# A fourth seven-product pair in seven feed-forward units, three low halves added by DMA, later transposes and a longer load ring

## The chip, the cores and the metric

One core of a Trainium2 chip runs the whole program. The metric is the device time of one execution in microseconds (us); the median of the runs of the kernel before is 1593.85 us (three runs, 1590.32 to 1594.32). The engines are called as in the profile: PE (matrix products, with PEld for its weight loads), DVE (vector), ACT (scalar functions), POOL (GpSimd) and SP, which here only issues DMAs. Each of them runs its instructions in the order in which the program puts them, and waits at an instruction until what it needs is there.

## The reference

A transformer layer over 256 rows of width 2048, in 32-bit floats: a normalisation with shift, scale and gate from a conditioning vector `c`, three token mixers over one projection, an output projection, and a gated feed-forward part of width 5632.

```python
mod = silu(c) @ w_ada + b_ada
shift1, scale1, gate1, shift2, scale2, gate2 = split(mod, 6)
h = rms_norm(x, norm1_gain) * (1 + scale1) + shift1
x = x + gate1 * mixing_sublayer(h, ...)     # stick-breaking, dilated, gated linear attention
h = rms_norm(x, norm2_gain) * (1 + scale2) + shift2
gate, up = split(h @ w_ffn_in, 2)
x = x + gate2 * ((silu(gate) * up) @ w_ffn_out)
```

## The kernel before

**Products.** Every 32-bit operand is split into a high part of reduced precision and the remainder, its low half. A product is three matmuls (`mm3`, lines 162 to 166): high by high, high by low (line 165, which reads the low half of the weights), low by high. A matmul has 128 rows of depth, 128 rows of the activation and 512 columns of weights.

**Weights.** A tile of weights is 256 rows by 512 columns, 512 KB. SP loads it into a raw room (four of them, tag `raw`). ACT casts it to the high part (line 158 in `load_weights`, 1305 in `split` of `load_pair`), and DVE subtracts the high part from the raw tile to give the low half (lines 159 and 1306). These results go to four rooms `whi`/`wlo`; in units 1 to 7 of the feed-forward part two more pairs of rooms (`more_rooms`, the tags A2/A3 and A4/A8, shown as A) join them, in a fixed rotation of six. A room is free again when PE has read it, a raw room when ACT and DVE have.

**The feed-forward part.** It runs in 11 units of 512 gate columns and the 512 up columns that belong to them; the depth of 2048 is taken as 8 pairs of 128-row chunks. Units 0 and 8 to 10 take the gate columns first and then the up columns, by `block`. Units 1 to 7 (`FAST`) take both at once in `fast_products`, pair by pair in the order of `PAIRS`. A plain pair p (flag 0) has a tile of gate and a tile of up columns (here "first tile" and "second tile"), and 8 products: 24 matmuls, in the order of the columns. A pair with flag 1, called fast here, treats the 2x2 blocks of activations (two row tiles by two chunks) and weights (two chunks by two column halves) by a scheme of seven products in place of eight, 21 matmuls. For it DVE makes four differences of weights in two further rooms, tags OD and KD (line 1309), and three and a half tiles are cast and split. The activations' differences that a fast pair needs are made once, in unit 0 (`sums_of_h2`). Four of the seven products go to shared PSUM banks over all fast pairs of a unit. After the last fast pair ACT and DVE combine them (lines 1380 to 1384) and DVE adds the combinations to the four outputs (`merge`, line 1340). Plain pairs behind the last fast pair add to the same outputs.

Behind a unit, ACT takes the sigmoid of the gate half (line 1419), DVE multiplies (lines 1420 and 1429), and in the next unit, between its first and its second pair, PE transposes the result with eight small matmuls (`turn`, line 1119), ACT and DVE splitting it for the last stage. The unit's two groups of PSUM banks, acc and misc, change places from unit to unit.

Below, P0 to P4 are plain pairs, and F5 to F7 fast ones. Before: P0, P1, F5, P2, F6, F7, P3, P4.

**Mixers.** `qk_norm` scales the heads of queries and keys on DVE (line 646), and `qk_turn` transposes them on PE (line 658) with a copy by ACT (line 659). For the stick-breaking heads this happens in one go after block 5 of the projection, and the first scores (line 681) follow in `gla`, by `sb_step`, between the chunks of blocks 9 to 12. For the dilated heads it happens in steps of a block: `steps` names the chunk before which each step is put. `dil_scores` makes the scores (with an exp on ACT, line 891), `mixture` transposes the probabilities on PE (line 936), and a sigmoid of the gates stands in between on ACT, which loads another function table for it.

**Gate2.** From unit 8 on, the products of `c` with the columns of `w_ada` for gate2 run in the background, paced by `tick`. SP loads 512 KB at a time into a ring of rooms (`ring["tags"]`, three: AR0, AR1, KC), and DVE multiplies and adds (line 289). `mac` keeps at most as many loads open as the ring has rooms. The middle sum x2 is kept in DRAM meanwhile: POOL stores it by four DMAs of 512 KB in the stage before (`put_away`, line 1217), and SP brings it back into A2, A3, A4 and A8 (`bring_back`, line 1221) once the fast units are through. In the last stage (`w_ffn_out`) fast pairs are used too.

**Order.** A scheduler puts the instructions on their engines by a priority that follows the program; `prio()` raises it for loads, casts and the like, so that these come ahead. `tc.issue_after(x)` puts an instruction behind x on its engine.

Of the kernel before, what the change touches and what calls it, by code (L numbers as in the profile page):

```python
# [10 lines left out]
F32 = mybir.dt.float32  # L11
F32R = mybir.dt.float32r
U8 = mybir.dt.uint8
AF = mybir.ActivationFunctionType
ALU = mybir.AluOpType
AX = mybir.AxisListType

P = 128
T = 256
NT = T // P  # L20
D = 2048
KC = D // P
DFF = 5632
NB = 512
# [8 lines left out]
RATE_IN, RATE_MID, RATE_FFN = 0.8, 0.6, 0.65  # L33
RATE_OUT = 2.5
LOOK = 3
DEFER = 4
AHEAD = 4000
WARM = (22, 38, 13)
# [7 lines left out]
OUT_UNITS = (4, 5, 6)  # L46
OUT_A = tuple((p, 0) for p in range(8)) + tuple(x for i in range(6) for x in ((8 + i, 1), (14 + i, 0))) + ((20, 0), (21, 0))
OUT_B = ((0, 0), (1, 0)) + tuple(x for i in range(6) for x in ((8 + i, 1), (2 + i, 0)))
PAIRS = ((0, 0), (1, 0), (5, 1), (2, 0), (6, 1), (7, 1), (3, 0), (4, 0))
RANK = 16  # L50
ROW_N1, ROW_N2, ROW_SBQ, ROW_SBK, ROW_DILQ, ROW_DILK, ROW_GB, ROW_GG = 16, 32, 48, 49, 50, 51, 52, 56

# [23 lines left out]
def trunk(ctx: ExitStack, tc: tile.TileContext, I, out):  # L76
# [16 lines left out]
    def S(tag, shape, dtype=F32):  # L93
        return slot.tile(shape, dtype, tag=tag, name=nm(tag))
# [383 lines left out]
    def proj_block(g, b, w=None, carry=False, steps=None):  # L478
        k0, k1 = GROUPS[g]
        go_on = bool(carried)  # L480
        pss = carried.pop() if go_on else [acc_bank() for _ in range(NT)]
        seeded = g == LAST and not go_on
        if seeded:

            with prio():
                for t in range(NT):
                    nc.scalar.copy(pss[t], A[b][:, t, :])
            go_on = True
        block(pss, h_at, w_in, k0, k1, b * NB, w=w, go_on=go_on, more=carry, seeded=seeded, steps=steps)
# [160 lines left out]
    def qk_turn(parts, behind=None):  # L650

        for b, h0, h1, gain in parts:
            for h in range(h0, h1, 2):
                ps = misc_bank([P, NT, 2, P])
                for t in range(NT):
                    for i in range(2):
                        with tc.issue_after(behind) if behind is not None else nullcontext():
                            nc.tensor.transpose(ps[:, t, i, :], heads(b)[:, t, h + i, :], ident)
                nc.scalar.activation(heads(b)[:, :, h : h + 2, :], ps, AF.Copy, scale=gain(h))
# [62 lines left out]
    def gla():  # L722
# [19 lines left out]
        nc.scalar.copy(aT, ps[: 2 * RANK, :])  # L742

        for i, b in enumerate((9, 10, 11, 12)):
            proj_block(LAST, b, steps={1: lambda: sb_step(2 * i), 3: lambda: sb_step(2 * i + 1)})
        with tc.issue_after(state["mm"].ins), prio():
            sb_step(8)

# [264 lines left out]
        proj_block(LAST, b)  # L1013
    state["rate"] = RATE_IN
    proj_block(LAST, 5)
    qk_turn(sb_parts, state["mm"].ins)
    sb_hi, sb_lo, sb_step = stick_breaking()
    og = gla()
    for b in range(6, 9):
# [5 lines left out]

    dil_scores, dil_weights = dilated()
    dil_steps = {
        4: lambda: qk_turn(dil_parts[:2]),
        7: lambda: qk_turn(dil_parts[2:]),
        10: lambda: dil_scores(0, 3),  # L1030
        13: lambda: dil_scores(3, 6),
    }
    rr = []
    for j in range(2):
# [228 lines left out]
    def sums_of(sf, h, a, b):  # L1263

        (a0, b0), (a1, b1) = ((x[:, a, :], x[:, b, :]) for x in h)
        for dst, x, y, op in (
            (0, a1, b1, ALU.add), (2, a0, a1, ALU.subtract), (1, sf[:, 0], a0, ALU.subtract), (3, b0, sf[:, 1], ALU.subtract)
        ):
            nc.vector.tensor_tensor(sf[:, dst], x, y, op=op)

    def sums_of_h2():
        out = {}
        sf = S("AR1", [P, 4, P])
        sums_of(sf.rearrange("p s (n d) -> p s n d", n=1), [h2_raw[2, t] for t in range(NT)], slice(2, 3), slice(3, 4))
        hl = S("AR0", [P, 2, 4, P], F32R)
        nc.scalar.copy(hl[:, 0], sf)
        nc.vector.tensor_tensor(hl[:, 1], sf, hl[:, 0].bitcast(F32), op=ALU.subtract)
        out[5] = [(hl[:, 0, j, :], hl[:, 1, j, :]) for j in range(4)]
        sf = S("AR1", [P, 4, 2, P])
        sums_of(sf, [h2_raw[3, t] for t in range(NT)], slice(0, 4, 2), slice(1, 4, 2))  # L1280
        hi, lo = S("OS1", [P, 4, 2, P], F32R), S("OS2", [P, 4, 2, P], F32R)
        nc.scalar.copy(hi, sf)
        nc.vector.tensor_tensor(lo, sf, hi.bitcast(F32), op=ALU.subtract)
        for n in range(2):
            out[6 + n] = [(hi[:, j, n, :], lo[:, j, n, :]) for j in range(4)]
        return out

    def load_pair(src, p, c0, c1, fast, tags):


        def raw_at(c):
            raw = wp.tile([P, 2, NB], F32, tag="raw", name=nm("raw"))
            nc.sync.dma_start(raw, src[2 * p * P : (2 * p + 2) * P, c : c + NB].rearrange("(k p) c -> p k c", p=P))
            return raw

        def split(src):
            n = src.shape[1]
            more_rooms = state.get("more_rooms", ())
            i = state["tiles"] = (state.get("tiles", -1) + 1) % (4 + len(more_rooms))
            if i < len(more_rooms):  # L1300
                hi, lo = (S(tag, [P, 2, NB], F32R) for tag in more_rooms[i])
            else:
                hi = wp.tile([P, 2, NB], F32R, tag="whi", name=nm("whi"), bufs=4)
                lo = wp.tile([P, 2, NB], F32R, tag="wlo", name=nm("wlo"), bufs=4)
            nc.scalar.copy(hi[:, :n, :], src)  # L1305
            state["split"] = nc.vector.tensor_tensor(lo[:, :n, :], src, hi[:, :n, :].bitcast(F32), op=ALU.subtract)  # L1306
            return [(hi[:, i, :], lo[:, i, :]) for i in range(n)]

        sub = lambda dst, x, y: nc.vector.tensor_tensor(dst, x, y, op=ALU.subtract)
        with prio():  # L1310
            if not fast:
                return [split(raw_at(c0)), split(raw_at(c1))]
            r0, r1 = raw_at(c0), raw_at(c1)
            b11, b21 = split(r0)
            ta, tb = (S(tag, [P, 2, NB]) for tag in tags)
            sub(ta[:, 0], r1[:, 0], r0[:, 0])
            sub(ta[:, 1], r1[:, 1], r1[:, 0])
            (b22,) = split(r1[:, 1:2])
            sub(tb[:, 0], r1[:, 1], ta[:, 0])
            sub(tb[:, 1], r0[:, 1], tb[:, 0])  # L1320
            t1, t3 = split(ta)
            t2, t4 = split(tb)
            return b11, b21, b22, t1, t3, t2, t4
# [68 lines left out]
        return fast_products(w_ff, i * NB, DFF + i * NB, PAIRS, h2_at, h2s, own, other, ("OD", "KD"))  # L1392

    state["rate"] = RATE_FFN
    state["more_rooms"] = tuple(zip(X2_TAGS[0::2], X2_TAGS[1::2]))
    ring["tags"] = ("AR0", "AR1", "KC")
    act = []
    for i in range(NFF):
        if i in FAST:
            pg, pu = fast_unit(i)  # L1400
        else:
            pg = [acc_bank() for _ in range(NT)]
        if i == FAST[-1] + 1:
            bg.append(gate2_bg())
        if i in FAST:
            pass
        elif i == 0:
            w = load_weights(w_ff, 0, KC, 0, spare=("A12", "KD", "A9", "A10", "A0", "A1", "T1", "T2"))
            for t in range(NT):
                block(pg, h2_at, None, 0, KC, 0, w=w, tiles=(t,), steps=None if t else {N2_AT[1]: lambda: norm2_turn(1, xs)})  # L1410
        else:
            block(pg, h2_at, w_ff, 0, KC, i * NB)
        if i == 0:
            h2s = sums_of_h2()
        sgs = []
        with prio():
            for t in range(NT):
                sg = scr([P, NB])
                nc.scalar.activation(sg, pg[t], AF.Sigmoid)
                nc.vector.tensor_mul(sg, sg, pg[t])  # L1420
                sgs.append(sg)
        if i not in FAST:
            pu = [acc_bank() for _ in range(NT)]
            block(pu, h2_at, w_ff, 0, KC, DFF + i * NB)
        hi = S(ftags[2 * i], [P, 4, T], F32R)
        lo = S(ftags[2 * i + 1], [P, 4, T], F32R)
        with prio():
            for t in range(NT):
                nc.vector.tensor_mul(sgs[t], sgs[t], pu[t])  # L1429

        def turn(sgs=sgs, hi=hi, lo=lo, bank=acc_bank if i + 1 in FAST and i % 2 == 0 else misc_bank):
            for t in range(NT):
                transpose_split(sgs[t], hi, lo, t, bank)

        later.append(turn)
        act.append((hi, lo))
# [33 lines left out]


    state["rate"] = RATE_OUT
    state["more_rooms"] = ()
    hooks = {at: (lambda n=n: sums_of_unit(n)) for n, at in enumerate((2, 4, 6))}
    hooks[7] = flush

# [84 lines left out]
```

## Time and profile before

| | us |
|---|---|
| median of the runs (1590.32 to 1594.32) | 1593.85 |
| the profiled execution | 1593.15 |
| its span, first to last instruction | 1591.4 |
| PE busy | 1576.3 |
| DVE busy | 1299.3 |
| ACT busy | 850.2 |
| POOL busy | 11.2 |

The times of the page are those of the profiled execution; 1.75 us of its time lie outside the span. The granted clock of PE is at or above nine tenths in every slice of it. A PE matmul is shown with its whole duration of 0.39 us, though the next one starts 0.23 us after it; its pace is read from the starts. A row of groups gives the line, the engine, what is written and read, the shape, the count, the busy time and the mean in ns, and then the engine's idle time ahead of such instructions and what ended it.

### The profile page before, as it was taken

The page shows a single profiled execution, that of the slowest core. Times are in us where ns is not written, and L with a number is a line of the kernel's source. Part 1 is how long each engine was busy: PE and PEld are TensorE (multiplying, and loading weights), DVE is VectorE, ACT ScalarE, POOL GpSimd, SP SyncE. Part 2 cuts the span into 40 slices and gives each one's busy share as a digit, 9 for nine tenths or more (in the row PEclk, how much of TensorE's full clock was granted, in tenths as well). Part 3 has the DMA queues.
Part 4 walks back from the last instruction along what each step waited for, and adds up shares of the span by engine and source line. Part 5 has one row for each costly group of instructions (what it writes and reads, how often), then busy time and mean ns, then how long its engine had stood idle before and what let it go on. Part 6 is the DMA issues. An engine that isn't in the chain of part 4 may idle for free.

```text
span 1591.4 us, 20176 instructions
## 1 busy us (share of the span) xinstructions
PE 1576.3 (99%) x7243; PEld 1304.6 (82%) x7243; DVE 1299.3 (82%) x1556; ACT 850.2 (53%) x1193; POOL 11.2 (1%) x22
## 2 busy tenths in 40 slices
PE   8999999999999999999999999999999999999998
PEld 7878888888788888888887888888888888888887
DVE  6889996888888686877756689999997777989884
ACT  5654448775755444444445755555554444455552
POOL 1000000000000000000000000000000000000000
PEclk9999999999999999999999999999999999999999
DMA  9999997667788899988767556666668889756664
GB/s 330 357 331 322 332 305 235 220 193 248 233 273 271 297 306 316 317 283 293 230 210 240 179 185 196 194 202 196 211 189 276 283 294 313 244 185 218 205 206 139
DMA packets 195740, 400.16 MB, mean 251 GB/s; under 512 B 13038, under 2 KB 28052, under 8 KB 195640
## 3 DMA queue, kind: packets, MB, share of 16 engines
q1 hardware_dynamic: 194664, 396.70, 75.6%
q0 software_dynamic: 800, 2.11, 0.3%
q8 instruction: 57, 0.93, 0.3%
q14 instruction: 43, 0.35, 0.1%
q10 hardware_dynamic: 176, 0.07, 0.0%
HBM read 394.63 MB, written 4.19 MB: 251 GB/s over the span
## 4 chain that ended last, share of the span: by engine, by line
PE 86%; DMA 5%; DVE 5%; ACT 3%; issue 1%; SPq 0%; ACTq 0%; DVEq 0%
PE acc L166 21%; PE acc L165 21%; PE acc L164 21%; PE misc L165 6%; PE misc L166 6%; PE misc L164 6%; DMA raw<-w_ffn_out 1%; DMA AR<-w_ada 1%; DVE ada L289 1%; ACT whi L158 1%; DVE wlo L159 1%; PE misc L809 1%; DMA A<-w_ada 1%; DMA OS<-w_ada 1%; DVE wlo L1306 1%
## 5 line engine op out<-in xcount | busy, mean ns | idle before, releaser
L158 ACT CAST whi<-raw 128x1024 fp32r<-128x1024 f32 x362 | 368.6, 1022 | 411.0 <-PE acc L166 257.2
L159 DVE TENSOR_TENSOR wlo<-raw,whi 128x1024 fp32r<-128x1024 f32 x362 | 426.2, 1184 | 181.3 <-ACT whi L158 179.0
L164 PE MATMUL acc<-whi,H 128*128 128x512 f32 x1245 | 487.3, 392 | 1.4 <-ACT H L455 0.8
L165 PE MATMUL acc<-wlo,H 128*128 128x512 f32 x1245 | 486.5, 391 | 0.8 <-DVE wlo L159 0.7
L166 PE MATMUL acc<-whi,H 128*128 128x512 f32 x1245 | 485.2, 390 | 0.4 <-DVE H L462 0.4
L166 PEld LDWEIGHTS acc<-whi,H 128*128 128x128 f32 x1245 | 233.5, 188 | 50.6 <-DVE H L462 1.6
L164 PEld LDWEIGHTS acc<-whi,H 128*128 128x128 f32 x1245 | 233.7, 188 | 50.2 <-ACT H L455 1.3
L165 PEld LDWEIGHTS acc<-wlo,H 128*128 128x128 f32 x1245 | 233.8, 188 | 48.7 <-DVE wlo L159 1.7
L1305 ACT CAST whi<-raw 128x1024 fp32r<-128x1024 f32 (+1 forms) x148 | 141.9, 974 | 99.8 <-PE acc L166 40.1
L1306 DVE TENSOR_TENSOR wlo<-raw,whi 128x1024 fp32r<-128x1024 f32 (+1 forms) x148 | 162.6, 1122 | 8.1 <-ACT whi L1305 6.8
L164 PE MATMUL acc<-whi,A 128*128 128x512 f32 x222 | 87.0, 392 | 1.0 <-DVE scr L1429 1.0
L165 PE MATMUL acc<-wlo,A 128*128 128x512 f32 x222 | 86.4, 389 | 0.0
L166 PE MATMUL acc<-whi,A 128*128 128x512 f32 x216 | 84.1, 389 | 0.0
L289 DVE SCALAR_TENSOR_TENSOR ada<-AR,csil,ada 128x1024 f32<-128x1024 f32 x60 | 76.1, 1280 | 7.3 <-DMA AR<-w_ada 7.3
L165 PE MATMUL misc<-wlo,H 128*128 128x512 f32 x158 | 61.7, 390 | 0.8 <-DVE wlo L1306 0.8
L164 PE MATMUL misc<-whi,H 128*128 128x512 f32 x158 | 61.7, 391 | 0.0
L166 PE MATMUL misc<-whi,H 128*128 128x512 f32 x158 | 61.5, 389 | 0.0
L164 PEld LDWEIGHTS acc<-whi,A 128*128 128x128 f32 x222 | 41.7, 188 | 9.8 <-issue 1.4
L165 PEld LDWEIGHTS acc<-wlo,A 128*128 128x128 f32 x222 | 41.7, 188 | 8.6 <-DVE wlo L159 0.2
L1305 ACT CAST whi<-AR 128x1024 fp32r<-128x1024 f32 x24 | 25.3, 1053 | 43.6 <-PE acc L166 21.1
L1305 ACT CAST A<-raw 128x1024 fp32r<-128x1024 f32 (+1 forms) x36 | 34.9, 982 | 25.0 <-PE misc L166 8.6
L166 PEld LDWEIGHTS acc<-whi,A 128*128 128x128 f32 x216 | 40.5, 188 | 8.5
(485 smaller groups left out, 2291.0 us busy)
## 6 DMA issues: line engine op xcount, KB each, us to landing
raw<-w_in SPq DMA_DIRECT2D x205, 512.0 KB, 5.2
raw<-w_ffn_in SPq DMA_DIRECT2D x176, 512.0 KB, 4.5
raw<-w_ffn_out SPq DMA_DIRECT2D x88, 512.0 KB, 4.9
AR<-w_ada SPq DMA_DIRECT2D x79, 512.0 KB, 5.0
raw<-w_out SPq DMA_DIRECT2D x32, 512.0 KB, 4.9
KC<-w_ada SPq DMA_DIRECT2D x30, 512.0 KB, 5.2
OS<-w_ada SPq DMA_DIRECT2D x16, 512.0 KB, 6.9
KD<-w_ada SPq DMA_DIRECT2D x16, 512.0 KB, 5.5
```

Of the source, the lines that this page charges most:

```text
L158: state["cast"] = nc.scalar.copy(hi[:, :n, :], raw[:, :n, :])
L159: state["split"] = nc.vector.tensor_tensor(lo[:, :n, :], raw[:, :n, :], hi[:, :n, :].bitcast(F32), op=ALU.subtract)
L164: nc.tensor.matmul(ps, lh, rh, start=start, stop=False, skip_group_check=seeded)
L165: nc.tensor.matmul(ps, lh, rl, start=False, stop=False, skip_group_check=seeded)
L166: state["mm"] = nc.tensor.matmul(ps, ll, rh, start=False, stop=stop, skip_group_check=seeded)
L289: nc.vector.scalar_tensor_tensor(acc, raw, c, acc, op0=ALU.mult, op1=ALU.add)
L809: nc.tensor.matmul(ps[:n, t * N_GLA + h, :].rearrange("p (s l) -> p s l", l=L), at(f, h, t)[:, :n], odd(at(f, h, t)), start=True, stop=True,)
L1305: nc.scalar.copy(hi[:, :n, :], src)
L1306: state["split"] = nc.vector.tensor_tensor(lo[:, :n, :], src, hi[:, :n, :].bitcast(F32), op=ALU.subtract)
```

## The change

It has four parts.

1. Pair 4 becomes a fast pair in units 1 to 7. The order is now P0, P1, F4, P2, F5, F6, F7, P3, so three fast pairs stand in a row and one plain pair behind them. Both merges come after the last pair. `sums_of_h2` also makes the activations' differences for pair 4.
2. The second tile of P0 and both tiles of P1 in units 1 to 7 get their low halves in another way: ACT writes the negated high part into the room of the low half, and POOL issues a DMA that reads the raw weights from DRAM again and adds them there. DVE has no part in these three tiles. These are 21 DMAs of 512 KB.
3. Transposes are held: the last of three groups of stick-breaking heads (eight transposes and two copies) is moved into block 9, and the two transposing steps of the dilated heads go from chunks 4 and 7 to 7 and 10, behind the product last issued, their scores from 10 and 13 to 13 and 15.
4. The ring of gate2 loads has five rooms instead of three; A2 and A3 join it, so these two quarters of x2 come back later.

```diff
-PAIRS = ((0, 0), (1, 0), (5, 1), (2, 0), (6, 1), (7, 1), (3, 0), (4, 0))
+PAIRS = ((0, 0), (1, 0), (4, 1), (2, 0), (5, 1), (6, 1), (7, 1), (3, 0))
+ADDED = ((0, True), (1, False), (1, True))
...
         for i, b in enumerate((9, 10, 11, 12)):
-            proj_block(LAST, b, steps={1: lambda: sb_step(2 * i), 3: lambda: sb_step(2 * i + 1)})
+            steps = {1: lambda: sb_step(2 * i), 3: lambda: sb_step(2 * i + 1)}
+            if i == 0:
+                steps[2] = lambda: qk_turn(sb_parts[2:], state["mm"].ins)
+            proj_block(LAST, b, steps=steps)
...
-    qk_turn(sb_parts, state["mm"].ins)
+    qk_turn(sb_parts[:2], state["mm"].ins)
...
     dil_steps = {
-        4: lambda: qk_turn(dil_parts[:2]),
-        7: lambda: qk_turn(dil_parts[2:]),
-        10: lambda: dil_scores(0, 3),
-        13: lambda: dil_scores(3, 6),
+        7: lambda: qk_turn(dil_parts[:2], state["mm"].ins),
+        10: lambda: qk_turn(dil_parts[2:], state["mm"].ins),
+        13: lambda: dil_scores(0, 3),
+        15: lambda: dil_scores(3, 6),
     }
...
     def sums_of_h2():
         out = {}
-        sf = S("AR1", [P, 4, P])
-        sums_of(sf.rearrange("p s (n d) -> p s n d", n=1), [h2_raw[2, t] for t in range(NT)], slice(2, 3), slice(3, 4))
-        hl = S("AR0", [P, 2, 4, P], F32R)
...
+        for n in range(2):
+            sf = S("OD", [P, 4, P])
+            c = 2 * n
+            sums_of(sf.rearrange("p s (n d) -> p s n d", n=1), [h2_raw[2, t] for t in range(NT)], slice(c, c + 1), slice(c + 1, c + 2))
+            hl = S(f"AR{n}", [P, 2, 4, P], F32R)
+            nc.scalar.copy(hl[:, 0], sf)
+            nc.vector.tensor_tensor(hl[:, 1], sf, hl[:, 0].bitcast(F32), op=ALU.subtract)
+            out[4 + n] = [(hl[:, 0, j, :], hl[:, 1, j, :]) for j in range(4)]
+        sf = S("KC", [P, 4, 2, P])
...
+        def weights(c):
+            return src[2 * p * P : (2 * p + 2) * P, c : c + NB].rearrange("(k p) c -> p k c", p=P)
...
-        def split(src):
+        def split(src, again=None):
...
             nc.scalar.copy(hi[:, :n, :], src)
-            state["split"] = nc.vector.tensor_tensor(lo[:, :n, :], src, hi[:, :n, :].bitcast(F32), op=ALU.subtract)
+            if again is None:
+                state["split"] = nc.vector.tensor_tensor(lo[:, :n, :], src, hi[:, :n, :].bitcast(F32), op=ALU.subtract)
+            else:
+                nc.scalar.activation(lo, hi.bitcast(F32), AF.Copy, scale=-1.0)
+                nc.gpsimd.dma_start(lo, again, accum_op=ALU.add)
...
-                return [split(raw_at(c0)), split(raw_at(c1))]
+                return [split(raw_at(c), weights(c) if (p, c == c1) in state.get("added", ()) else None) for c in (c0, c1)]
...
     state["rate"] = RATE_FFN
+    state["added"] = ADDED
...
         if i == FAST[-1] + 1:
+            ring["tags"] = ("AR0", "AR1", "KC", "A2", "A3")
             bg.append(gate2_bg())
...
-    state["more_rooms"] = ()
+    state["more_rooms"] = state["added"] = ()
```

More of the change, by code (lines that the diff above doesn't have):

```diff
@@ L1272, in sums_of_h2 @@
         out = {}
-        sf = S("AR1", [P, 4, P])
-        sums_of(sf.rearrange("p s (n d) -> p s n d", n=1), [h2_raw[2, t] for t in range(NT)], slice(2, 3), slice(3, 4))
-        hl = S("AR0", [P, 2, 4, P], F32R)
[L1276 to L1279, printed above, removed]
+        for n in range(2):
[7 more added lines that the diff above has]
+        sf = S("KC", [P, 4, 2, P])
         sums_of(sf, [h2_raw[3, t] for t in range(NT)], slice(0, 4, 2), slice(1, 4, 2))
@@ L1288, in load_pair @@
     def load_pair(src, p, c0, c1, fast, tags):
+        def weights(c):
+            return src[2 * p * P : (2 * p + 2) * P, c : c + NB].rearrange("(k p) c -> p k c", p=P)
         def raw_at(c):
             raw = wp.tile([P, 2, NB], F32, tag="raw", name=nm("raw"))
-            nc.sync.dma_start(raw, src[2 * p * P : (2 * p + 2) * P, c : c + NB].rearrange("(k p) c -> p k c", p=P))
+            nc.sync.dma_start(raw, weights(c))
             return raw
-        def split(src):
+        def split(src, again=None):
             n = src.shape[1]
```

## The prediction

> **What bounds the kernel now.** I read the page first (busy times, chain), then PE's waits, the chain over units 1 to 7, the windows of one unit, the groups of DVE and ACT.
>
> ```profile
> span 1591.4 us, 20176 instructions
> ...
> PE 1576.3 (99%) x7243; PEld 1304.6 (82%) x7243; DVE 1299.3 (82%) x1556; ACT 850.2 (53%) x1193; POOL 11.2 (1%) x22
> ...
> PE 86%; DMA 5%; DVE 5%; ACT 3%; issue 1%; SPq 0%; ACTq 0%; DVEq 0%
> ```
>
> PE sets the end: only fewer matmuls, or shorter waits of PE, can bring time. Its waits, as total, count and longest:
>
> ```profile
> PE misc L658 <- DVE A L646: 1.8, 2, 1.1
> PE acc L164 <- DVE scr L1429: 1.0, 1, 1.0
> PE misc L658 <- ACT A L659: 0.9, 1, 0.9
> ...
> PE misc L165 <- DVE wlo L1306: 0.8, 1, 0.8
> ```
>
> None of these lies in units 1 to 7 (926.0 to 1222.7 us). There the chain is PE alone, and seven units end on the beat:
>
> ```profile
> 1010.81 0.87 PE acc L1119 x8
> ...
> 1053.18 0.87 PE misc L1119 x8
> ...
> 1222.73 0.88 PE misc L1119 x8
> ```
>
> A unit takes (1222.73 - 1010.81)/5 = 42.38 us: the turn of 0.87, and 3 fast pairs of 21 matmuls and 5 plain ones of 24, 183 in all, so 0.2268 us each. The window of one unit shows how close the others are (busy us of PE, PEld, DVE, ACT, POOL, then clock, DMA share, GB/s):
>
> ```profile
> 1010.80:1053.20 42.40, 42.40 (x194) 35.20 (x192) 39.71 (x49) 24.12 (x27) 0.00 (x0) 1.00 0.63 198
> ```
>
> DVE is busy for 39.71 us of 42.40, at a granted clock of 1.00. It is the next bound, 2.7 us away.
>
> **The change, part by part.** *Seven products for a fourth pair.* Each of seven units loses 3 matmuls: 21 x 0.2268 = **-4.76 us** if PE never waits; the unit becomes 41.70. The price is on DVE and ACT (count, busy, mean ns):
>
> ```profile
> L1306 DVE TENSOR_TENSOR wlo<-raw,whi 128x1024 fp32r<-128x1024 f32 x58 | 69.8, 1220 | 4.9 <-ACT whi L1305 4.9
> ...
> L1309 DVE TENSOR_TENSOR OD<-raw,raw 128x512 f32<-128x512 f32 x20 | 13.8, 688 | 4.7 <-DMA raw<-w_ffn_in 4.7
> ```
>
> ```profile
> L1305 ACT CAST whi<-raw 128x1024 fp32r<-128x1024 f32 x58 | 60.7, 1054 | 44.0 <-PE misc L166 15.6 <-PE acc L166 13.0 <-DMA raw<-w_ffn_in 9.1
> ```
>
> Back to back these overlap a little, so I cost DVE from start to start: 1.14 us for 1024 columns, 0.60 for 512.
>
> ```profile
> 1089.65 1.22 DVE L1306 TENSOR_TENSOR wlo<-raw,whi 128x1024 fp32r<-128x1024 f32 x1
> 1090.79 0.69 DVE L1340 TENSOR_TENSOR acc<-acc,KC 128x512 f32<-128x512 f32 x1
> 1091.39 0.68 DVE L1420 TENSOR_TENSOR scr<-scr,acc 128x512 f32<-128x512 f32 x1
> ```
>
> A fast pair needs three splits of 1024 and five operations of 512 (four differences, one split), 6.42 us; a plain one two splits, 2.28. That is +4.14 per unit. *The adding DMAs* take 3 splits (-3.42) away. DVE then has 39.71 + 0.72 = 40.43 us of work in a unit of 41.70: 1.27 us left, where it had 2.69. ACT gets one and a half casts more and three negated copies, 4.5 x 1.05 = 4.7, so 28.9 of 41.7: off the path by its sum, though each copy stands between a cast and POOL's issue.
>
> What decides is the adding DMA's time from issue to landing, L. No row shows one that adds. The nearest are POOL's four plain stores of the same 512 KB, and SP's loads of the same tiles in one unit:
>
> ```profile
> L1217 POOL DMA_DIRECT2D x<-A x4: 531/534/568, 809.6 to 876.3; - x4
> ...
> DMA to landing us min/median/max: 2.9/5.4/6.2
> ```
>
> ```profile
> L1293 SPq DMA_DIRECT2D raw<-w_ffn_in x19: 367/368/372, 1000.7 to 1046.2; - x19
> ...
> DMA to landing us min/median/max: 3.6/4.4/5.0
> ```
>
> ```profile
> q1 hardware_dynamic: 194664, 396.70, 75.6%
> ```
>
> The stores' landings follow what else is under way; their stretches (0.84 is the DMA share of the 6.2 us from 831.37, 0.61 that of the store of 2.9):
>
> ```profile
> 831.40:837.60 6.20, 6.20 (x30) 5.11 (x28) 2.94 (x3) 2.96 (x5) 0.51 (x1) 1.00 0.84 273
> ...
> 876.30:879.30 3.00, 3.00 (x15) 2.49 (x14) 1.02 (x2) 3.00 (x10) 0.53 (x1) 1.00 0.61 243
> ```
>
> A packet takes 0.756 x 16 x 1591.4 / 194664 = 0.099 us; 512 KB are 256 packets of 2 KB, 16 for each engine, 1.58 us. An add has the tile in SBUF to read as well. Bounds: 2.9 (the fastest store, the second read hidden) and 6.2 + 1.6 = 7.8 (the slowest, the second read wholly added). A unit's share grows from 0.63 to 0.63 x 19/16 = 0.75 (three tiles more than 16), between the two stores. I take 5.2: the median load of these units, 4.4, which lies between them too, and half of the second read.
>
> The budget, counted from the end of the last fast pair (F7): P3 runs to 5.45, P0 of the next unit to 10.9, the turn to 11.77, P1 to 17.2. Plain pairs take the columns in order, so the second tile's low half is read half-way: P0's at 8.4, P1's at 14.7, and P1's first at 12.0. P0's second raw tile is issued when F7's differences free its room, at -3.5, lands at about 0.8 (4.4 later), is cast by 1.85, negated by 2.95, issued at 3.05: it has 5.35 us. P1's first, issued at 5.75, has 6.2. P1's second negation stands on ACT behind both sigmoids and is issued between 9.0 and 9.9: 4.8 to 5.7. So the smallest budget is 4.8 to 5.35, and one us of L beyond it costs PE one us in each of six units (unit 1 loads these tiles while plain unit 0 runs). With L = 5.2 the stall is 0 to 0.4; I take 0.2 x 6 = **+1.2**; ends 0 and (7.8 - 5.2) x 6 = 15.6. SP's raw loads share the engines with these tiles: 198 GB/s become about 235, less than the 312 of the window from 1312 us below, where PE was still busy for 44.04 of 45.00; 0.
>
> What is queued behind: PE runs in order, so everything behind P0 or P1 slips with it. POOL has nothing else in these units. The tiles free their rooms only when PE has read them, so a stall also holds back the casts six tiles on; it doesn't add up.
>
> The Trainium skill, "DMA: Bandwidth & Descriptors", section "Anatomy of one DMA — SWDGE (gpsimd) path", fits a fixed 2.0 us plus bytes over 436 GB/s, an estimate of 3.2 us here: by it the sum has no stall. The row of 2.9 agrees, the median of 5.4 does not.
>
> *Three fast pairs in a row, one plain pair behind.* In before, DVE is ahead of PE in the last fast pair by 3.3 us: the split ends at 1074.62, and PE reads it at 1077.95.
>
> ```profile
> 1073.40 1.22 DVE L1306 TENSOR_TENSOR wlo<-KD,whi 128x1024 fp32r<-128x1024 f32 x1
> ```
>
> ```profile
> 1077.95 0.39 PE L165 MATMUL misc<-wlo,OS 128*128 128x512 f32 x1
> ```
>
> A fast pair takes PE 4.76 and DVE 6.42, so each in a row eats 1.66 of the lead: the third leaves 3.3 - 1.66 = 1.6, less what the fuller tiles hold back; following the six rooms step by step I get 0.7. Positive, so 0; the bound is in the rivals. The last product (L1429) ends 2.1 us before the turn needs it; by the same steps, 0.7; also 0.
>
> ```profile
> 1092.58 0.68 DVE L1429 TENSOR_TENSOR scr<-scr,acc 128x512 f32<-128x512 f32 x1
> ```
>
> ```profile
> 1095.41 1.04 PE L1119 MATMUL acc<-ident,scr 128*128 128x128 f32 x8
> ```
>
> *Held transposes.* For the stick-breaking heads:
>
> ```profile
> 277.32 1.84 ACT L659 ACTIVATE A<-misc,qgains 128x512 f32<-128x512 f32 x3
> ...
> 279.04 1.85 ACT L659 ACTIVATE A<-misc,vec 128x512 f32<-128x512 f32 x3
> ```
>
> ```profile
> 278.06 1.24 PE L658 MATMUL misc<-ident,A 128*128 128x128 f32 x8 [0.94 <-ACT A L659]
> ...
> 279.83 0.66 PE L681 MATMUL misc<-A,A 128*128 128x256 f32 x2
> ```
>
> The last eight transposes go behind the first two chunks of block 9, but the first scores (L681, at 279.83) need the fourth copy, which is among the first four that stay and ends at 279.04 + 1.85/3 = 279.7 either way. PE comes there sooner and waits there: the wait moves. 0, within 0.9 either way. For the dilated heads both transposes go 3 steps later, and L646's results (ready 1.1 us late at worst) are there:
>
> ```profile
> 413.62 0.39 PE L166 MATMUL acc<-whi,H 128*128 128x512 f32 x1
> 415.10 0.44 PE L658 MATMUL misc<-ident,A 128*128 128x128 f32 x2 [1.10 <-DVE A L646]
> ```
>
> -1.8. The scores come 17 matmuls later, and ACT's exp for them now falls behind a sigmoid with two more table loads of 1.28 us:
>
> ```profile
> 441.67 1.28 ACT L1071 ACT_TABLE_LOAD   x1
> ```
>
> The probabilities' transposes are only 78 matmuls behind the scores, instead of 84. So 0 to 1.3 us come back; I take 0.4: **-1.4**.
>
> *Two more rooms for gate2.*
>
> ```profile
> 1351.08 1.29 DVE L289 SCALAR_TENSOR_TENSOR ada<-AR,csil,ada 128x1024 f32<-128x1024 f32 x1 [1.54 <-DMA AR<-w_ada]
> 1352.28 1.22 DVE L1306 TENSOR_TENSOR wlo<-raw,whi 128x1024 fp32r<-128x1024 f32 x1
> 1353.42 1.28 DVE L1429 TENSOR_TENSOR scr<-scr,acc 128x512 f32<-128x512 f32 x2
> ```
>
> DVE idles 1.54 for a load that had no room earlier; L1429 behind it is what PE waited 1.0 for. Earlier loads take that away: -1.0. Against it, the engines there are at 0.92, and two halves of x2 come back later, between SP's loads of w_ffn_out:
>
> ```profile
> 1312.00:1357.00 45.00, 44.04 (x197) 36.21 (x195) 34.75 (x34) 18.92 (x20) 0.00 (x0) 1.00 0.92 312
> ```
>
> Bounds -1.0 and +1.6 (one tile's 1.58 before a raw tile); nearer the first: **-0.8**.
>
> **Sum.** -4.76 + 1.2 + 0 - 1.4 - 0.8 = -5.8. The profiled execution took 1593.15 (the span and 1.75 around it): 1587.4. The median of the runs shown is 0.7 above it: **1588.1**.
>
> **Rivals.** *A, the add lands late (slower).* Place: the low halves of P0 and P1 in units 2 to 7. Price: L - 5.2 six times. Without stalls the sum is -7.0, so it is used up at L = 6.4, and from 7.2 on the kernel is slower by over 0.3%; at 7.8, 15.6 - 7.0 gives 1602.5. For it: the store at a share of 0.84 took 6.2, and adds come in pairs with raw loads. Against: the loads of these very units never exceed 5.0, and the share stays below 0.84.
>
> *B, a full second read.* L = 4.4 + 1.6 = 6.0: 0.8 x 6 = 4.8, so 1593.85 - 7.0 + 4.8 = 1591.7, within 0.3%. Packets of the q1 row speak for it, their idle third of the time against. The Trainium skill, "Collectives: The Full Stack", section "The bandwidth ceiling: the fold count and why AG ≠ RS ≠ AR", says that an add reads two sources and halves the rate; no run here shows that.
>
> *C, DVE becomes the bound.* If it keeps its 2.69 us of idle in each unit (waits for casts and raw tiles, as the group rows show), a unit takes 43.12, +1.42 over 41.70, x 6 = 8.5 instead of 1.2: 1595.4, no difference. For it: the leads of 0.7. Against: much of that idle is slack that shrinks when DVE is late.
>
> *D, the waits only move.* Held transposes and rooms give 0: 1590.3.
>
> **How the numbers follow.** 0.3% (4.8 us) is about what a measurement of this kernel can tell from no change: faster is below 1589.1, slower above 1598.6. Forecast 0.50, A 0.22, B 0.10, C 0.10, D 0.08. The forecast's own range is 1585.4 (no stall, -1.8, -1.0, and 0.9 more at L681) to 1590.5 (twice the stall, half of the last two gains: 1588.1 + 1.2 + 1.1). By these, the forecast gives 0.42 to faster and 0.08 to no change; A (L from 6.4 to 7.8) 0.06 to no change and 0.16 to slower; B 0.02 to faster and 0.08 to no change; C 0.06 to no change and 0.04 to slower; D 0.03 to faster and 0.05 to no change. Faster 0.47, same 0.33, slower 0.20. Range 1584.5 to 1602.
>
> **What would show it.** PE's waits in units 2 to 7: none, or a few tenths at L165 of P0 and P1, put down to POOL's DMA; turns 41.7 to 42.0 us apart; landing of the POOL DMAs 4.5 to 5.5; DVE's share of a unit at 96%; L658 no longer waiting for L646; 1.54 at L289 gone. I am wrong if the turns lie 42.5 or more apart (A by POOL's landings, C if PE waits for L1306), or if the waits of L658 and L1429 turn up again at L681, L941 or in the last stage.

## The result and the profile after

The changed kernel takes 1635.76 us (median of 4 runs, 1634.19 to 1636.69), the kernel before 1593.54 beside it: a ratio of 1.0262, 95% interval 1.025 to 1.0274. It is 42 us slower; 1588.1 was forecast, and 1602 was the upper end.

On the page of the changed kernel, these are the counterparts of the lines shown of before:

```profile
span 1634.1 us, 20254 instructions
...
PE 1587.4 (97%) x7222; PEld 1306.8 (80%) x7222; DVE 1305.9 (80%) x1582; ACT 880.7 (54%) x1231; POOL 36.7 (2%) x43
...
q0 software_dynamic: 6512, 13.12, 4.1%
...
PE 76%; DMA 9%; DVE 6%; ACT 5%; issue 4%; POOL 0%; SPq 0%; ACTq 0%; DVEq 0%; POOLq 0%
```

PE has 21 matmuls fewer and is busy for 11 us more; the chain is PE for 76% and no longer 86%, and DMA has 9% of it in place of 5. PE's waits in the changed kernel (total, count, longest) name the DMAs:

```profile
PE misc L167 <- DMA A<-w_ffn_in: 13.0, 4, 4.4
PE acc L167 <- DMA A<-w_ffn_in: 12.9, 3, 4.6
PE acc L167 <- DVE wlo L161: 4.6, 3, 3.2
...
PE misc L167 <- DMA wlo<-w_ffn_in: 1.3, 2, 0.7
```

Loads from `w_ffn_in` straight into a low half (A is the room A4/A8) are the adds. Seven waits of the second tile of P0, one for each unit, are 25.9 us. The line of the adds in the changed kernel (ns of the instruction, then the landing of all 21):

```profile
L1321 POOL DMA_DIRECT2D A<-w_ffn_in x7: 1194/1203/1263, 914.4 to 1207.0; - x7
...
DMA to landing us min/median/max: 9.0/10.1/12.7
```

L, taken as 5.2 and bounded by 7.8, is 9.0 at its least. The timelines of POOL and PE over one such wait show where it falls:

```profile
1013.93 1.20 POOL L1321 DMA_DIRECT2D A<-w_ffn_in  x1 [40.51 <-ACT A L1320]
```

```profile
1018.41 0.39 PE L166 MATMUL misc<-A,H 128*128 128x512 f32 x1
1023.21 0.80 PE L167 MATMUL misc<-A,H 128*128 128x512 f32 x1 [4.41 <-DMA A<-w_ffn_in]
1023.80 0.63 PE L168 MATMUL misc<-A,H 128*128 128x512 f32 x1
1024.23 0.63 PE L166 MATMUL misc<-A,H 128*128 128x512 f32 x1
...
1026.37 0.53 PE L168 MATMUL misc<-A,H 128*128 128x512 f32 x1
1026.73 0.40 PE L166 MATMUL misc<-A,H 128*128 128x512 f32 x1
```

The add is issued at 1013.93, and PE wants the tile 0.23 behind 1018.41: a budget of 4.7 us. In the six units 2 to 7 this budget is 4.6 to 5.4 us, and the add lands after 9.0 to 10.0. Behind the wait the matmuls start 0.43 us apart in place of 0.23. The windows around it (busy us of PE, PEld, DVE, ACT, POOL, then granted clock, DMA share, GB/s) say why:

```profile
1013.90:1018.40 4.50, 4.50 (x21) 3.74 (x20) 3.82 (x7) 4.45 (x6) 2.40 (x2) 1.00 1.05 316
1018.40:1023.20 4.80, 0.40 (x2) 0.00 (x0) 4.15 (x7) 1.97 (x4) 1.20 (x1) 1.00 1.08 258
1023.20:1026.40 3.20, 3.19 (x8) 2.54 (x9) 1.28 (x3) 0.00 (x0) 0.00 (x0) 0.50 1.10 258
1026.40:1030.00 3.60, 3.60 (x21) 3.08 (x20) 1.32 (x3) 1.94 (x3) 0.00 (x0) 0.97 1.02 255
```

```profile
1027.40:1075.40 48.00, 43.81 (x190) 35.59 (x189) 40.53 (x51) 28.12 (x32) 3.61 (x3) 0.96 0.73 204
```

The clock granted after the pause is 0.50 for 3.2 us. That adds some 2 us to every wait, and the page puts it under "PE busy". The DMA share counts each packet with its whole time in the window where it starts, so it can pass 1. It is above 1.0 throughout, though it is 0.73 over a unit (the last row).

Where the 42 us lie can be read from the turns of units 0 to 7: 927.21, 978.99, 1027.43, 1075.37, 1123.11, 1172.98, 1220.27 and 1265.92. Those seven intervals take 338.7 us, 42.0 more than the 296.7 of before, whose first of these turns is this one (the last was shown at 1222.73):

```profile
926.02 0.87 PE acc L1119 x8
```

The span as a whole is 42.7 us longer. Against 7 x 41.70 = 291.9 the seven are 46.8 too long. By the starts of the matmuls this divides into:

```
second tile of P0, six waits (units 2 to 7)         26.5
slower matmuls behind them                          12.5
unit 8, its first splits (L161)                      3.4
adds for P1                                          2.3
splits and casts of fast pairs (L1317, L1315)        2.1
```

### The profile page after: what moved, and what is told of

It reads as the page before. It is cut to its first block, busy times and chain, and to the rows that moved or that the text cites. A ratio compares the mean times of both kernels' runs of the same rounds, so it can differ in the third digit from the quotient of the medians.

```text
span 1634.1 us, 20254 instructions
## 1 busy us (share of the span) xinstructions
PE 1587.4 (97%) x7222; PEld 1306.8 (80%) x7222; DVE 1305.9 (80%) x1582; ACT 880.7 (54%) x1231; POOL 36.7 (2%) x43
## 3 DMA queue, kind: packets, MB, share of 16 engines
q0 software_dynamic: 6512, 13.12, 4.1%
## 4 chain that ended last, share of the span: by engine, by line
PE 76%; DMA 9%; DVE 6%; ACT 5%; issue 4%; POOL 0%; SPq 0%; ACTq 0%; DVEq 0%; POOLq 0%
PE acc L167 19%; PE acc L168 19%; PE acc L166 19%; PE misc L167 4%; PE misc L168 4%; PE misc L166 4%; DMA A<-w_ffn_in 2%; DMA wlo<-w_ffn_in 2%; DVE wlo L1317 2%; DMA raw<-w_ffn_in 1%; ACT whi L160 1%; DMA raw<-w_in 1%; DVE wlo L161 1%; ACT whi L1315 1%; DMA raw<-w_br_gla 1%
## 5 line engine op out<-in xcount | busy, mean ns | idle before, releaser
L1315 ACT CAST whi<-raw 128x1024 fp32r<-128x1024 f32 (+1 forms) x156 | 146.7, 959 | 76.2 <-PE misc L168 22.2
L1317 DVE TENSOR_TENSOR wlo<-raw,whi 128x1024 fp32r<-128x1024 f32 (+1 forms) x142 | 152.8, 1095 | 10.2 <-ACT whi L1315 8.5
L291 DVE SCALAR_TENSOR_TENSOR ada<-AR,csil,ada 128x1024 f32<-128x1024 f32 x51 | 64.8, 1278 | 2.9 <-DMA AR<-w_ada 2.9
L167 PEld LDWEIGHTS acc<-wlo,A 128*128 128x128 f32 x222 | 41.7, 188 | 9.5 <-DVE wlo L161 1.1
L166 PEld LDWEIGHTS acc<-whi,A 128*128 128x128 f32 x222 | 41.7, 188 | 9.3 <-ACT whi L160 0.8
L168 PE MATMUL acc<-whi,OS 128*128 128x512 f32 x107 | 41.7, 389 | 0.0
```

The source lines that it names most:

```text
L166: nc.tensor.matmul(ps, lh, rh, start=start, stop=False, skip_group_check=seeded)
L167: nc.tensor.matmul(ps, lh, rl, start=False, stop=False, skip_group_check=seeded)
L168: state["mm"] = nc.tensor.matmul(ps, ll, rh, start=False, stop=stop, skip_group_check=seeded)
L291: nc.vector.scalar_tensor_tensor(acc, raw, c, acc, op0=ALU.mult, op1=ALU.add)
```

## The experiments

### e1 to e4: the adds or the pairs

Four kernels, each with one edit of the changed one. e1: no adds, DVE splits everything.

```diff
-ADDED = ((0, True), (1, False), (1, True))
+ADDED = ()
```

> The changed kernel with DVE making all low halves, no adding DMAs; everything else as changed. Theory (the adds land 9 us and later, PE waits 4.1 to 4.8 us for the second tile of P0 and then runs 4 us at half clock): those waits and the half clock vanish; what is left is DVE with 39.71 + 0.72 + 3.42 = 43.85 us of work in a unit of 41.70, so about 2.1 us in each of seven units: 1593.5 - 5.5 + 15 = about 1603, no PE wait for a DMA in units 1 to 7. Rival (three fast pairs in a row and one plain pair behind them starve PE whoever makes the low halves): 1625 or more, with long waits of PE at the first pairs of each unit.

e2: the DMAs only write the raw weights; the kernel leaves out the addition.

```diff
-                nc.gpsimd.dma_start(lo, again, accum_op=ALU.add)
+                nc.gpsimd.dma_start(lo, again.bitcast(F32R))
```

> The same 21 DMAs from POOL's queue, behind the same negations, but writing the raw weights in place of adding them; the low halves of three tiles are then the raw weights themselves. Theory (the add is what makes the DMA slow): the packets fall from 0.18 to about 0.1 us, the landing from 9.0-12.7 to 4.5-6.5 us, PE waits at most 1.5 us per unit, 1588 to 1598. Rival (any DMA of this size from POOL's queue is this late beside the raw loads): landing stays above 8 us and the time above 1625.

e3: POOL subtracts.

```diff
-                nc.scalar.activation(lo, hi.bitcast(F32), AF.Copy, scale=-1.0)
-                nc.gpsimd.dma_start(lo, again, accum_op=ALU.add)
+                nc.gpsimd.tensor_tensor(lo[:, :n, :], src, hi[:, :n, :].bitcast(F32), op=ALU.subtract)
```

> The low halves of the three tiles are made by a subtraction on POOL from the raw tile, no second load, no negation; pairs, transposes and rooms as changed. Theory: no PE wait for a DMA in units 1 to 7. No row shows such a subtraction on POOL; if it takes up to 4 us and leaves DVE's 1.22 us alone, PE keeps its beat and the time is 1586 to 1591; if it takes longer, or DVE's splits become longer beside it, 1595 to 1620. Rival (three fast pairs in a row starve PE): 1625 or more.

e4: the old pairs.

```diff
-PAIRS = ((0, 0), (1, 0), (4, 1), (2, 0), (5, 1), (6, 1), (7, 1), (3, 0))
+PAIRS = ((0, 0), (1, 0), (5, 1), (2, 0), (6, 1), (7, 1), (3, 0), (4, 0))
```

> The changed kernel with the pairs of before (three fast pairs, the order of before), the three adding DMAs kept. Theory (the adds cost the time by themselves): PE still waits for them, 3 to 5 us a unit and the half clock behind each wait: 1615 to 1640. Rival (only with four fast pairs is there no time left for the adds): 1590 to 1597, no wait over 1 us.

| run | us | ratio to before | 95% interval |
|---|---|---|---|
| e1, DVE splits all | 1627.11 | 1.0217 | 1.0202 to 1.0232 |
| e2, plain write | 1613.91 | 1.0132 | 1.0091 to 1.0173 |
| e3, POOL subtracts | 1610.84 | 1.0120 | 1.0104 to 1.0137 |
| e4, old pairs, adds kept | 1621.27 | 1.0180 | 1.0165 to 1.0196 |

None confirms one theory alone. e4 shows that the adds cost time by themselves: +1.8% with the old pairs, where they land in 9.2 to 13.3 us. But e3, without any adding DMA, is still slower by 1.2%, where the sum without stalls had it faster by 7 us. Its PE waits are others:

```profile
PE misc L167 <- DVE wlo L1317: 3.8, 6, 0.8
...
PE acc L167 <- DVE wlo L1317: 3.6, 6, 0.8
PE acc L1124 <- DVE scr L1445: 1.7, 3, 0.6
```

DVE's and PE's timelines of e3 show the place, the last fast pair of a unit:

```profile
1084.39 1.22 DVE L1317 TENSOR_TENSOR wlo<-OD,whi 128x1024 fp32r<-128x1024 f32 x1
1085.53 0.69 DVE L1323 TENSOR_TENSOR KD<-raw,KD 128x512 f32<-128x512 f32 x1
1087.41 1.23 DVE L1317 TENSOR_TENSOR wlo<-KD,whi 128x1024 fp32r<-128x1024 f32 x1 [1.19 <-ACT whi L1315]
```

```profile
1085.67 0.50 PE L167 MATMUL misc<-wlo,OS 128*128 128x512 f32 x1 [0.31 <-DVE wlo L1317]
...
1087.43 0.49 PE L166 MATMUL misc<-whi,OS 128*128 128x512 f32 x1 [0.33 <-ACT whi L1315]
```

The split of OD ends at 1085.61, and PE begins with it at once; the split of KD behind it, from 1087.41 to 1088.64, is waited for in the same way. No lead is left (for KD it was 3.3 us). The last difference stands behind the split of OD on DVE, its cast behind the difference, its split behind the cast. So DVE itself idles 1.19 us just where it is late.

e2 separates the add from the transfer. Its landings, again of all 21:

```profile
L1321 POOL DMA_DIRECT2D A<-w_ffn_in x7: 713/713/730, 910.7 to 1188.8; - x7
...
DMA to landing us min/median/max: 5.2/8.0/9.4
```

```profile
q0 software_dynamic: 6512, 13.12, 2.4%
```

The plain write of the same tiles takes 8.0 us in the middle; the add makes that 10.1. The packets of 21 DMAs (6512 - 800 = 5712 in both kernels) take (4.1% - 0.3%) x 16 x 1634.1 / 5712 = 0.174 us each with the add, and (2.4% - 0.3%) x 16 x 1612.6 / 5712 = 0.095 without. So the add nearly doubles the time of a packet, and the landing is 2 us later. The larger part of the error, 8.0 in place of 4.4, is in the plain transfer. The windows of e2 over its first landing in a unit:

```profile
1004.20:1008.70 4.50, 4.50 (x21) 3.72 (x21) 4.24 (x8) 4.02 (x5) 1.41 (x2) 1.00 0.95 315
1008.70:1011.80 3.10, 0.93 (x5) 0.43 (x3) 2.27 (x4) 2.51 (x4) 0.71 (x1) 1.00 1.16 390
```

The engines are full there, because three of SP's raw loads are under way beside two of POOL's transfers. These loads are late as well:

```profile
L1303 SPq DMA_DIRECT2D raw<-w_ffn_in x3: 368/368/368, 1003.7 to 1007.9; - x3
...
DMA to landing us min/median/max: 5.7/7.0/7.3
```

Their median was 4.4 in the kernel before, and the four that the changed kernel issues from 1012.6 to 1017.5 land after 5.9 to 10.1. So what is late isn't POOL's queue, the rival put down for e2, but every transfer in this stretch. An estimate from the prediction's 1.58 us for one tile: five tiles take 5 x 1.58 = 7.9 us. With two adds among them, at 256 x 0.174 / 16 = 2.8 us each, they take 10.3. Without the row of three (e9, below) the share in this stretch is the same, 1.05 and 1.10.

e1 prices DVE as the bound. In one interval between turns it has work for 43.63 of 46.72 us, as reckoned (43.85), but PE loses 5.0 and not DVE's excess of 2.1, because DVE is idle for 3.1 us of it as well:

```profile
1063.73:1110.45 46.72, 43.10 (x187) 33.62 (x186) 43.63 (x55) 25.45 (x29) 0.00 (x0) 1.00 0.56 181
```

### e7 to e9: DVE's work or the row of three

e7 gives all eight plain tiles of a unit to POOL, which relieves DVE by five more splits (e3 otherwise).

```diff
-ADDED = ((0, True), (1, False), (1, True))
+ADDED = tuple((p, c) for p in range(4) for c in (False, True))
```

> The changed kernel, the low halves of all eight tiles of the plain pairs of units 1 to 7 by subtraction on POOL (2.4 us each in e3, 19 us of a unit), no adding DMAs. Theory (DVE's work around the row of three fast pairs is what e3 still lost 3.2 us a unit by): DVE has 40.4 - 5.7 = 34.7 us of a unit, PE's waits for L1317 fall below 0.5 a unit, 1586 to 1593 with the unit 8 wait. Rival (the order of the row, ACT's casts and the six rooms set it, not DVE's work): 1604 or more.

e8 is e3 with no three fast pairs in a row.

```diff
-PAIRS = ((0, 0), (1, 0), (4, 1), (2, 0), (5, 1), (6, 1), (7, 1), (3, 0))
+PAIRS = ((0, 0), (1, 0), (4, 1), (5, 1), (2, 0), (6, 1), (7, 1), (3, 0))
```

> e3 (three low halves on POOL) with the pairs in the order P0, P1, F4, F5, P2, F6, F7, P3: no three fast pairs in a row. Theory (the third fast pair in a row outruns DVE, 6.4 us of work against 4.8 of PE): waits at F7 vanish, 1590 to 1598. Rival (DVE's total of 40.4 us in 41.7 sets it, or the order behind the last fast pair): 1605 to 1612, as e3.

e9 is the changed kernel, adds and all, with e8's line of pairs.

> The changed kernel with its adding DMAs, the pairs in the order of e8 (P0, P1, F4, F5, P2, F6, F7, P3). What the adds cost where the row of three no longer does. Theory (an add lands 9 to 12 us after its issue and PE, with 5 us to spare, waits 4 or more for the first of three, then runs at half pace): 1612 to 1630, landings of 9 us and more. Rival (the adds are late only because the row of three holds their tiles back): at most 1600.

| run | us | ratio to before | 95% interval |
|---|---|---|---|
| e7, eight tiles on POOL, row of three | 1623.46 | 1.0190 | 1.0174 to 1.0206 |
| e8, three tiles on POOL, no row of three | 1591.84 | 0.9994 | 0.9984 to 1.0003 |
| e9, adds, no row of three | 1612.23 | 1.0111 | 1.0086 to 1.0137 |

e8 settles the row: the same work in another order is 19 us faster than e3. A window of each, 42.00 us in the units of e8 and 100 us in those of e7:

```profile
1010.00:1052.00 42.00, 41.71 (x188) 34.28 (x187) 39.90 (x52) 24.51 (x29) 7.26 (x3) 1.00 0.62 200
```

```profile
1000.00:1100.00 100.00, 92.34 (x395) 71.30 (x395) 83.06 (x98) 53.75 (x63) 44.99 (x19) 1.00 0.56 178
```

In e8 DVE works for 95% of the window and PE keeps its beat there. From turn to turn e8 takes 41.7, 41.7 and 41.8 us, then 42.6, 42.4 and 42.3, and 46.4 up to the first pair of unit 8. So DVE's total does not set the 44.9 of e3, and rival C, with its 43.12 by DVE's sum, had the wrong mechanism.

e7 is no clean test of it. DVE is busy for 83% there and PE is slower than in e8 by far, but POOL and DVE hold each other up:

```profile
1010.16 4.80 POOL L1320 TENSOR_TENSOR wlo<-raw,whi 128x1024 fp32r<-128x1024 f32 x2
```

```profile
1010.64 1.28 DVE L1445 TENSOR_TENSOR scr<-scr,acc 128x512 f32<-128x512 f32 x2
1012.68 3.37 DVE L1317 TENSOR_TENSOR wlo<-raw,whi 128x1024 fp32r<-128x1024 f32 x1 [0.76 <-ACT whi L1315]
```

The split takes 3.37 us in place of 1.22 and ends 1.09 us behind POOL's subtraction; the two products of L1445, which read `acc` in PSUM, keep their 0.68. Around units 1 to 7 of e7, 16 splits and differences of DVE are longer in this way, by 31 us in all, while its intervals are some 5.3 us over 41.70. In e3 and e8 no DVE instruction is longer beside POOL. PE also waits for L1320, 4.0 us in all.

e9 gives the adds their price in the better order: 20 us more than e8. Its longest wait for a tile of P0 is 2.6 us. In the unit shown it is 2.27, with the add issued earlier (at 1002.47 for a tile wanted at 1010.3, a budget of 7.9 us):

```profile
1002.47 1.20 POOL L1321 DMA_DIRECT2D A<-w_ffn_in  x1 [38.24 <-ACT A L1320]
```

```profile
1012.75 0.50 PE L167 MATMUL misc<-A,H 128*128 128x512 f32 x1 [2.27 <-DMA A<-w_ffn_in]
```

It still landed over 10 us after its issue. So the row of three took some 3 us of the adds' budget as well: the changed kernel, which has both, is 24 us slower than e9. By the ratios, the adds alone (e9 to e8) are 1.2% and the row alone (e3 to e8) 1.3%, both together 2.7%; what is left over is not clear of the noise.

### e5, e6: the two small parts alone

e5 is the kernel before with the change's edits to `gla`, `qk_turn` and `dil_steps`, e6 the kernel before with this:

```diff
+            ring["tags"] = ("AR0", "AR1", "KC", "A2", "A3")
             bg.append(gate2_bg())
```

> The kernel before with the held transposes alone. As the profile of the changed kernel shows these places (at the dilated transposes 0.2 us are lost in place of 2.1, 0.4 comes anew at the transposes of the probabilities, the stick-breaking wait is 0.55 in place of 1.1): -2.3 us, 1589.5 to 1591.5. Rival (waits only move): 1592 to 1594.

> The kernel before with the two further rooms for gate2 alone. Theory (SP meets the load into A2, which waits for PE to leave that room, ahead of the raw loads of unit 8, so a raw tile is late and PE waits 3 us there): +1 to +3 us, 1593 to 1595.5, a wait of 2 to 4 us in unit 8, the wait at 1352.9 gone. Rival (the wait in unit 8 comes from the single plain pair behind unit 7's last fast pair): no wait there, -1.1 us, about 1591.

e5: 1593.16 us, ratio 0.9998 (0.9989 to 1.0007), no difference. Its waits:

```profile
PE acc L164 <- DVE acc L1343: 0.8, 1, 0.8
...
PE misc L993 <- DVE T L988: 0.5, 1, 0.5
...
PE misc L939 <- DVE T L927: 0.2, 1, 0.2
```

The waits at the held transposes (L658, 2.7 us) are gone from the list, which now has these three, none of them among the waits quoted of before.

e6: 1590.24 us, ratio 0.9981 (0.9972 to 0.9990), faster by 3.1 us. The wait for L1429 is gone, and that for L1306 has shrunk from 0.8:

```profile
PE misc L165 <- DVE wlo L1306: 0.2, 1, 0.2
```

There is no wait in unit 8: the theory that the room A2 holds up SP there falls for the old pairs.

e6 also shows something of e5. It has no held transposes, and yet this is all that PE waits for at L658:

```profile
PE misc L658 <- DVE A L646: 0.3, 1, 0.3
```

Up to unit 8 PE, ACT and DVE have the same instructions in e6 as in before. So these waits come and go from one execution to the next, and the single profile of before does not show what holding the transposes can win. For the same reason 1.8 of the 3.1 us between the two profiled spans lie ahead of unit 0's turn (924.04 in e6, 925.86 in before), where e6's edit does nothing. At the edit's own place, between the last two turns, e6 takes 44.4 us; before, e5 and e11, which have three rooms, take 45.7, 45.0 and 46.2. From the last turn to the end, e6 and before both take 234.3.

### e10 to e12: the wait in unit 8

e8 still waits in unit 8 for a split that stands behind the sums of unit 7:

```profile
1219.96 0.50 PE L167 MATMUL acc<-wlo,H 128*128 128x512 f32 x1 [2.21 <-DVE wlo L161]
```

e10 is e8 with the longer ring one unit later, e11 with the old ring, e12 with the old pairs in unit 7 alone.

```diff
-        if i == FAST[-1] + 1:
+        if i == FAST[-1] + 2:
             ring["tags"] = ("AR0", "AR1", "KC", "A2", "A3")
+        if i == FAST[-1] + 1:
             bg.append(gate2_bg())
```

```diff
-            ring["tags"] = ("AR0", "AR1", "KC", "A2", "A3")
```

```diff
+LAST_PAIRS = ((0, 0), (1, 0), (5, 1), (2, 0), (6, 1), (7, 1), (3, 0), (4, 0))
...
-        return fast_products(w_ff, i * NB, DFF + i * NB, PAIRS, h2_at, h2s, own, other, ("OD", "KD"))
+        return fast_products(w_ff, i * NB, DFF + i * NB, PAIRS if i < FAST[-1] else LAST_PAIRS, h2_at, h2s, own, other, ("OD", "KD"))
```

> e8 with the five-room ring from unit 9 on, not from unit 8 on. Theory (the 2.4 us wait for L161 in unit 8 comes of the load into A2 that stands in SP's order ahead of unit 8's raw tiles): the wait falls below 1 us and the time to 1586 to 1590. Rival (it comes from the single plain pair behind unit 7's last fast pair, whose sums and sigmoids stand on DVE and ACT ahead of unit 8's splits): the wait stays, 1590 to 1593.

> e8 with three rooms for gate2 as before. Theory as for e10: no wait over 1 us in unit 8, but those at L1429's place in unit 9 and in the last stage (1.1 and 0.9 us) are back: 1588 to 1592. Rival (single plain pair): the wait in unit 8 stays, 1592 to 1595.

> e8 with unit 7 in the order of before (P0, P1, F5, P2, F6, F7, P3, P4: two plain pairs behind the last fast one), units 1 to 6 as in e8. Theory (unit 8's wait of 2.4 us comes of the single plain pair behind unit 7's last fast pair): the wait goes, three matmuls (0.7 us) come back: 1588 to 1590, below the kernel before and e8. Rival (it comes of the loads ahead of unit 8's raw tiles): the wait stays and the time is 1592 to 1593.

| run | us | ratio to before | 95% interval |
|---|---|---|---|
| e10, ring from unit 9 | 1590.63 | 0.9984 | 0.9973 to 0.9995 |
| e11, old ring | 1594.36 | 1.0003 | 0.9989 to 1.0017 |
| e12, old pairs in unit 7 | 1589.33 | 0.9976 | 0.9967 to 0.9986 |

The wait stays in e10 (2.4 us) and shrinks in e11 (1.3), so the ring is not what makes it, though it may add to it. In e12 no split of unit 8 is waited for by more than 0.7 us:

```profile
PE acc L168 <- DVE wlo L162: 1.4, 3, 0.7
```

So it is unit 7's order that makes the wait. Whether it is the single plain pair behind the last fast pair or the fourth fast pair itself stays open, since the order of before changes both. e12 is faster than the kernel before by 0.24% and than the changed one by 46 us. From e6 (0.9981) it can't be told apart.

## Why the prediction was wrong

- **The adding DMA's L: the step that failed.** "I take 5.2: the median load of these units, 4.4, which lies between them too, and half of the second read." It measured 9.0 to 12.7, outside the bounds too. The second read was sized about right (2.1 us of landing between e2 and the changed kernel, with 1.6 as its bound), the plain transfer was not: 8.0 where 4.4 was taken. I scaled the DMA share of a whole unit, 0.63 to 0.75 (it came out at 0.73), while the add is issued in a stretch at 1.05. The store of 6.2 us at a share of 0.84 was the nearer row, and still too short. That SP's raw loads share the engines with these tiles was put at 0, by the GB/s of a unit; beside the adds these loads too landed after up to 10.1 us.
- **Its price.** The step "one us of L beyond it costs PE one us in each of six units" held for the wait: 9.2 - 4.7 = 4.5 in the unit shown; and the budget of 4.8 to 5.35 came out (4.6 to 5.4). It left out the granted clock of 0.50 behind it, 12.5 / 6 = 2.1 us more each time. Rival A had the place, the mechanism and the sign; its 7.8 was too small an end.
- **Three fast pairs in a row.** The step "following the six rooms step by step I get 0.7. Positive, so 0" was the second failure: 19 us between e3 and e8. The plain sum, 3.3 - 1.66, had left 1.6; the order on DVE and ACT, where each difference, cast and split waits for the other engine, took all of it. I had reckoned a slack of 0.7 us out of a schedule by hand and then gave it a price of nothing. In the changed kernel the waits of this kind are only 2.1 us; while PE stands still for an add, DVE works on (4.15 of 4.80 us in the window shown).
- **DVE as the bound (rival C).** DVE's work came out as reckoned (40.53 us in a unit, forecast 40.43; ACT's is 28.1, and the printed 28.9 should be 24.12 + 4.7 = 28.8), but it did not decide: e8 has the same work and takes 41.7 to 42.6 us a unit, e3 44.9.
- **The matmuls.** The -4.76 were there in part: PE of e8 runs three units in a row from turn to turn in 41.7 to 41.8 us each, as forecast, but the next three in 42.3 to 42.6. These six save 1.7 us against before, where 4.1 were due, and the wait in unit 8 takes that back.
- **Held transposes.** -1.4 was forecast, 0.9998 measured, as rival D had it. The 1.8 us at L646 had been read from one execution, and in e6 they are 0.3 without the change.
- **Rooms for gate2.** -0.8 was forecast, e6 alone gives -3.1 (0.9972 to 0.9990). The place was right, and 1.2 us are seen there between before and e6. Where the rest comes from stays open: the other wait of the last stage (L1306) shrank too, but that stage is no shorter. In the changed kernel the wait in unit 8 outweighs the gain.

By the fit in the Trainium skill, "DMA: Bandwidth & Descriptors", section "Anatomy of one DMA — SWDGE (gpsimd) path", an estimate of 3.2 us, there would have been no stall; the runs show 5.2 at the least for a plain write on busy engines. The Trainium skill, "Collectives: The Full Stack", section "The bandwidth ceiling: the fold count and why AG ≠ RS ≠ AR", says of the reducing step of a ring of cores that its add needs two source reads and so runs at half the rate. The packets of this case agree: 0.174 against 0.095 us.

## What to carry to other kernels

Size a new transfer by the DMA share of the very stretch in which it is issued, not by that of the stage: count the transfers that will be under way beside it. Count also what PE loses in clock after a pause. Before a wait is given a price, see whether it stands in a second execution. Where one engine feeds another through a few rooms, the order of the dear steps matters before their sum does: spread those for which the feeder needs longer than the consumer, and treat a slack under 1 us from a hand schedule as none. A stage that moves work from a 95% busy engine to an idle one should first try the idle engine's own arithmetic before a DMA (e8 is 20 us faster than e9), and place it where the two don't meet: three subtractions a unit on POOL left DVE's 1.22 us as they were, eight did not.

## What the runs showed of the hardware

- The granted clock changes on a grid. In the changed kernel it falls to 0.50 at 972.0, 1023.2, 1071.0, 1118.8, 1166.6 and 1217.8 us, 14 or 15 times 3.413 us apart, for one or two such steps, and the matmuls then start 0.43 us apart. From 900 to 1270 us the seven runs with such falls have 22 of them. In the step ahead of each, PE was idle for 1.96 us or more; behind each of the 35 steps at full clock with 0.9 to 1.84 us of idle time, the clock stayed at 1.00. So what counts is the idle time within one step. In e9 a pause of 2.0 us inside one step halved the clock (the first two rows: PE's busy time, then the clock of the next step); in the changed kernel a pause of 3.2 us that falls on two steps did not (the last two rows, and the clock is 1.00 behind them):

```profile
963.57:966.99 3.42, 1.46 (x8) 0.88 (x6) 3.42 (x6) 1.10 (x2) 0.66 (x1) 1.00 1.10 274
966.99:970.40 3.41, 3.41 (x8) 2.65 (x9) 3.41 (x6) 1.05 (x1) 0.00 (x0) 0.50 1.10 259
```

```profile
1258.74:1262.15 3.41, 1.58 (x7) 0.96 (x6) 2.40 (x4) 2.60 (x4) 0.00 (x0) 1.00 0.90 305
1262.15:1265.57 3.42, 2.05 (x9) 1.72 (x10) 3.42 (x4) 0.00 (x0) 0.00 (x0) 1.00 0.48 137
```

The Trainium skill, "TensorE: Matmul & The Clock Gate", section "Part 1: The HAM clock gate (the "warmup" mystery)", puts it down to a free-running window of about 3.4 us without work, after which the clock is halved. The traces agree with the window, and show that some 2 us without work in it are enough.
- A POOL instruction that starts an adding DMA takes 1.20 us, a plain load 0.71, the plain stores 0.53.
- POOL's subtraction of 1024 columns takes 2.4 us for 14 of the 21 tiles of e3, 3.0 for the others, and DVE's own 1024-column splits stay at 1219 ns in e3. In e7, where the two engines meet, a split of DVE takes up to 3.5 us:

```profile
L1320 POOL TENSOR_TENSOR wlo<-raw,whi 128x1024 fp32r<-128x1024 f32 x14 | 33.3, 2400 | 1.1 <-ACT whi L1315 1.1
```

```profile
L1317 DVE TENSOR_TENSOR wlo<-raw,whi 128x1024 fp32r<-128x1024 f32 x48 | 57.3, 1219 | 0.0
```
